# A hybrid encoder layer: the last quarter's upper MLP layer by seven products of eight, with w_down's sums made a pass earlier on GpSimd

## The chip, the cores and the metric

The kernel runs on one core of one Trainium2 chip. The metric is the device time of one execution in microseconds (us), lower is better. The engines are named as in the profile: PE (TensorE matmul), PEld (its weight load), DVE (VectorE), ACT (ScalarE), POOL (GpSimd) and SP (SyncE, which here only issues DMAs).

## The reference, cut to what matters

One encoder layer on x of 2048 tokens by 1024 features, float32: an attention and a convolution side by side, a cross-attention to 256 memory rows, an MLP, a last norm.

```python
h = x + concat([dilated_attention(q, k, v), conformer_conv(a, g)]) @ w_out   # q,k,v,a,g = rmsnorm(x) @ w_in
h = h + cross_attention(rmsnorm(h), rmsnorm(mem)) @ w_xo
u = rmsnorm(h) @ w_up                  # 1024 -> 4096
h = h + square(relu(u)) @ w_down       # 4096 -> 1024
return rmsnorm(h)
```

## The kernel before

All large products run in float16 with each operand split into a high and a low part, so that one product is three matmuls (`mm3`, which is why three neighbouring lines, L374 to L376, hold nearly all of PE's time).

The tokens are cut into four quarters of 512 columns. `post(p)` is the work on quarter p: the output projection, the cross-attention, the MLP and the output; this text calls it a pass, first (p = 0) to last (p = 3). Beside passes 0 to 2, `weave` puts in the attention (`att`) and the convolution (`conv`, DVE's long chain of L391) of the next quarter. The passes are generators; a scheduler then sets the order in which each engine's instructions stand, and every engine takes its queue strictly in that order.

The MLP goes over eight groups (`fg`) of 512 hidden features. The upper layer (w_up) has two forms:
- plain: for each 128 features, 8 x 3 matmuls of 512 columns, 96 in a group (`hidden` in the last pass);
- `quad`: the group as a two by two block product by seven products instead of eight, 7 x 2 x 4 x 3 = 168 matmuls of 256 columns. It needs sums of blocks of w_up and of the activations. The activations' sums are made by `put_columns` when the cross-attention ends. Those of w_up are made once by `prep`, split in float16 and kept in DRAM (`ust`).

Before, groups 5 to 7 of the second pass and all groups of the third use `quad`; the last pass uses the plain form. `prep` runs as a side of the second and third pass (tables `preps`): for each group and each half j it loads two raw pieces of w_up (`pw`, 512 KB each) into buffers that the attention's result has left, makes four sums of 128x512 on DVE, splits everything (`hi` on ACT, `lo` on DVE) and writes the parts (`pt`) to DRAM. It is advanced by one step for each step of the main generator (rate 1.0).

The lower layer (w_down) of the last pass also goes by seven products (`seven`) for groups 0 to 6, with the hidden features' sums made by `parts` and w_down's sums (`sums`, on DVE, 128x1024) and splits (`piece`, ACT and DVE) made anew inside the last pass. In the other passes it is plain, with split weights that the first pass kept in DRAM (`wst`).

POOL does small jobs: the power function in each norm (`nr`, L347), the joining of the three attention patterns, and some DMA issues.

Of the kernel before, what the change touches and what calls it, by code (L numbers as in the profile page):

```python
# [21 lines left out]
P = 128  # L22
# [19 lines left out]
GV = {"mix": 0, "x": 8, "mlp": 16, "final": 24, "conv_b": 32, "ln_g": 36, "ln_b": 40}  # L42

# [5 lines left out]
def hybrid_layer(ctx, tc, A, out):  # L49
# [70 lines left out]
    ust = [[dr.tile([P, 2 * 1024], F16, name=f"ust{fg}_{i}") for i in range(7)] for fg in range(8)]  # L120
    vscr = dr.tile([P, 2, 8, 256], F16, name="vscr")
# [1392 lines left out]
    def prep(fgs):  # L1514
# [11 lines left out]
        def hi(o, i):  # L1526
            ACT.activation(o, i, AF.Copy, scale=S_UP)

        def lo(o, i, h):
            DVE.scalar_tensor_tensor(o, i, S_UP, h, op0=ALU.mult, op1=ALU.subtract)  # L1530

        for fg in fgs:
            for j in range(2):
# [3 lines left out]
                for i in range(2):  # L1537
                    dma(raw[i], wcols(w_up, (4 * fg + 2 * i + j) * P))
                a11, a12, a21, a22 = (r[:, 4 * i:4 * i + 4] for r in raw for i in range(2))
                yield  # L1540
# [4 lines left out]
                DVE.tensor_tensor(s1, a21, a22, op=ALU.add)  # L1545
                DVE.tensor_tensor(a21, a11, a21, op=ALU.subtract)
# [4 lines left out]
                DVE.tensor_tensor(a11, s1, a11, op=ALU.subtract)  # L1551
# [4 lines left out]
                DVE.tensor_tensor(a12, a12, a11, op=ALU.subtract)  # L1556
# [22 lines left out]
    preps = {1: (5, 6, 7, 3), 2: (4, 0, 1, 2)}  # L1579
# [46 lines left out]
    def quad(p, fg, src, hh, rsb):  # L1626
# [21 lines left out]
        def done(e, pt, i, z):  # L1648
# [5 lines left out]
            a, b = (t[:, 2 * i:2 * i + 2, 256 * z:256 * z + 256] for t in hh)  # L1654
            ACT.copy(a, e3)
            DVE.tensor_tensor(b, e3, a, op=ALU.subtract)  # L1656

        X, Y, Z = (ps(f"u{x}", "up") for x in "xyz")
# [16 lines left out]
        Y = ps("uy", "up")  # L1675
# [8 lines left out]
    def post(p):  # L1684
# [70 lines left out]
        if p in preps:  # L1755
            one, two_, src = columns(p)
            put = put_columns(one, two_, hs)
            y = None
        else:
            y = ytiles("m")  # L1760
# [15 lines left out]
        if p == 2:  # L1776
            opened = hidden_tiles(0, order[0])
            opened = (opened, quad(p, order[0], src, opened, rsb))
            next(opened[1])
        r = rstd_from(ssum)  # L1780
# [6 lines left out]
        if p == NG - 1:  # L1787
            last_mlp(hs, y, rsb)
            return
        for g in range(FG // 2):  # L1790
# [3 lines left out]
            for i, fg in enumerate(fgs):  # L1794
# [6 lines left out]
                if src and (p == 2 or fg > 4):  # L1801
                    while fg not in ready:
                        next(prepping[p])
                    yield from main_quad or quad(p, fg, src, ht, rsb)
# [59 lines left out]
    def last_mlp(hs, y, rsb):  # L1864
# [3 lines left out]
        banks.update(up=(4, 5, 6, 7), ux=(0, 1), uy=(2, 3), tr=(0, 1, 2, 3))  # L1868
# [225 lines left out]
```

## Time and profile before

| what | us |
|---|---|
| median of 3 runs | 2685.7 (2682.28 to 2688.09) |
| the profiled execution, whole | 2687.11 |
| its span, first to last instruction | 2685.3 |
| PE busy in the span | 2613.5 |
| DVE busy | 1982.5 |
| ACT busy | 1245.2 |
| POOL busy | 226.2 |

A row of a group of instructions reads: line, engine, operation, out<-in by the program's names, shapes, count, then busy time, mean ns of one, and the idle time before them. A row of a window reads: from and to, its length, and for each engine busy time and count, then granted clock, share of DMA engines in use and GB/s.

### The profile page before, as it was taken

To read this page: it belongs to the slowest core of one execution; us is meant where nothing else is said; L and a number is where in the kernel's file an instruction comes from. 1 tells how busy PE (TensorE), PEld (TensorE's weight loads), DVE (VectorE), ACT (ScalarE), POOL (GpSimd) and SP (SyncE) were. 2 spreads that over 40 slices of the span, in tenths; PEclk is the share of its full clock that TensorE was granted. 3 is DMA by queue.
4 is the path that set the end of the run, shared out by engine and by line. 5 is a ranking of instruction groups with operands and counts; after the bars stand their busy time and mean duration, and the time that the engine had idled before them with its cause. 6 is when DMAs were issued, how large, how long until landed. Compare 5 with 4: busy or idle time off the path is not lost.

```text
span 2685.3 us, 43789 instructions
## 1 busy us (share of the span) xinstructions
PE 2613.5 (97%) x16786; PEld 1561.7 (58%) x16786; DVE 1982.5 (74%) x3816; ACT 1245.2 (46%) x2189; POOL 226.2 (8%) x285
## 2 busy tenths in 40 slices
PE   8999999999899999999999999999999999999998
PEld 7844448766454555445576676555776565444443
DVE  5886656567679996556799985468999755677976
ACT  5637544476454345334552343256443343443433
POOL 1234002132001011100000000000000000000000
PEclk9999999999999999999999999999999999999999
DMA  9977978665526777855357777454787765323331
GB/s 270 296 259 215 286 227 268 176 194 169 164 85 180 231 218 217 267 183 166 118 161 227 216 233 235 126 159 124 234 272 255 232 227 157 102 71 102 114 114 63
DMA packets 445634, 510.97 MB, mean 190 GB/s; under 512 B 89613, under 2 KB 341441, under 8 KB 444656
## 3 DMA queue, kind: packets, MB, share of 16 engines
q1 hardware_dynamic: 438016, 493.15, 60.1%
q10 hardware_dynamic: 5184, 9.01, 0.9%
q0 software_dynamic: 2224, 6.01, 0.6%
q8 instruction: 132, 2.16, 0.3%
q14 instruction: 78, 0.64, 0.1%
HBM read 376.59 MB, written 131.48 MB: 189 GB/s over the span
## 4 chain that ended last, share of the span: by engine, by line
PE 75%; DVE 12%; DMA 6%; issue 3%; ACT 3%; SPq 1%; POOL 1%; DVEq 0%; POOLq 0%; ACTq 0%
PE dn L376 7%; PE dn L375 7%; PE dn L374 7%; PE up L374 6%; PE up L376 6%; PE up L375 6%; PE lin L376 3%; PE lin L374 3%; PE lin L375 3%; DVE cacc L391 3%; PE xs L375 2%; PE xs L376 2%; PE xs L374 2%; PE pt L1030 2%; PE x L375 2%
## 5 line engine op out<-in xcount | busy, mean ns | idle before, releaser
L391 DVE SCALAR_TENSOR_TENSOR cacc<-cu,cw,cacc 128x512 f32<-128x512 f32 x480 | 365.8, 768 | 5.0
L375 PE MATMUL dn<-hhl,ws_d 128*128 128x512 f16 x768 | 291.6, 380 | 1.4 <-DVE hhl L1656 1.1
L376 PE MATMUL dn<-hhh,ws_d 128*128 128x512 f16 x768 | 291.6, 380 | 0.0
L374 PE MATMUL dn<-hhh,ws_d 128*128 128x512 f16 x768 | 288.9, 380 | 1.0 <-ACT hhh L1821 0.4
L374 PE MATMUL up<-mh,ws_u 128*128 128x512 f16 x512 | 194.1, 380 | 0.9 <-ACT mh L1509 0.9
L375 PE MATMUL up<-ml,ws_u 128*128 128x512 f16 x512 | 194.5, 380 | 0.0
L376 PE MATMUL up<-mh,ws_u 128*128 128x512 f16 x512 | 194.4, 380 | 0.0
L1024 ACT ACTIVATE sm<-sm,o 128x256 f32<-128x256 f32 (+1 forms) x288 | 119.4, 455 | 130.7 <-DVE o L1023 130.2
L1023 DVE CUSTOM_DVE_ANT_0 sm<-s,mask,qks 128x256 f32<-128x256 f32 (+1 forms) x384 | 151.9, 436 | 34.4 <-PE s L1064 33.7
L1034 DVE TENSOR_TENSOR pl<-pt,ph 128x512 f16<-128x512 f32 x160 | 110.1, 688 | 41.2 <-ACT ph L1033 40.5
L1838 DVE SCALAR_TENSOR_TENSOR h<-dn,bd,h 128x512 f32<-128x512 f32 x96 | 71.7, 749 | 78.6 <-PE dn L376 76.9
L376 PEld LDWEIGHTS <-ws_d 128*128 128x128 f16 x768 | 75.3, 98 | 90.9 <-issue 2.1
L1033 ACT CAST ph<-pt 128x512 f16<-128x512 f32 x160 | 91.4, 572 | 77.7 <-PE pt L1030 77.5
L375 PEld LDWEIGHTS <-ws_d 128*128 128x128 f16 x768 | 75.2, 98 | 83.3 <-issue 0.8
L374 PEld LDWEIGHTS <-ws_d 128*128 128x128 f16 x768 | 75.3, 98 | 82.6 <-issue 0.7
L376 PEld LDWEIGHTS <-ws_u 128*128 128x128 f16 x832 | 81.7, 98 | 64.0 <-issue 0.6
L375 PEld LDWEIGHTS <-ws_u 128*128 128x128 f16 x832 | 81.6, 98 | 61.6 <-issue 0.9
L374 PEld LDWEIGHTS <-ws_u 128*128 128x128 f16 x832 | 81.6, 98 | 60.9 <-issue 0.6
L1030 PE MATMUL pt<-ident,sm 128*128 128x128 f32 x640 | 99.4, 277 | 9.0 <-DVE catl L1200 4.2
L376 PE MATMUL o<-cath,ws_o 128*128 128x512 f16 x256 | 97.3, 383 | 4.8 <-DVE ws_o L362 4.8
L1030 PEld LDWEIGHTS pt<-ident,sm 128*128 128x128 f32 x640 | 79.2, 143 | 35.0 <-ACT sm L1024 4.2
L374 PE MATMUL o<-cath,ws_o 128*128 128x512 f16 x256 | 97.3, 382 | 0.8 <-ACT cath L1199 0.7
(556 smaller groups left out, 7296.4 us busy)
## 6 DMA issues: line engine op xcount, KB each, us to landing
ws_t<-ust SPq DMA_DIRECT2D x77, 512.0 KB
ws_d<-wst SPq DMA_DIRECT2D x64, 512.0 KB
ws_u<-wst SPq DMA_DIRECT2D x52, 512.0 KB
ust<-pt SPq DMA_DIRECT2D x48, 512.0 KB
raw_d<-in_w_down_dram SPq DMA_DIRECT2D x36, 512.0 KB
scan<-in_w_up_dram SPq DMA_DIRECT2D x32, 512.0 KB
scan<-in_w_down_dram SPq DMA_DIRECT2D x32, 512.0 KB
raw_o<-in_w_out_dram SPq DMA_DIRECT2D x32, 512.0 KB
```

Of the source, the lines that this page charges most:

```text
L374: PE.matmul(o, lh, rh, start=first, stop=False, skip_group_check=more)
L375: PE.matmul(o, lh, rl, start=False, stop=False, skip_group_check=more)
L376: last["pe"] = PE.matmul(o, ll, rh, start=False, stop=end, skip_group_check=more)
L391: DVE.scalar_tensor_tensor(acc, u[:, t:t + 512], cw[:, c, t:t + 1], acc, op0=ALU.mult, op1=ALU.add)
L1023: last["dve"] = DVE.tensor_tensor_reduce(dst, so, mask[:, 256 * m:256 * m + nk], SCORE, 3e38, ALU.add, ALU.min, mn)
L1024: last["act"] = ACT.activation(dst, dst, AF.Exp, bias=mn, scale=-1.0)
L1030: last["pe"] = PE.transpose(pt[:, j, :], sm[:, j, :], ident)
L1033: ACT.copy(ph, pt)
L1034: DVE.tensor_tensor(pl, pt, ph, op=ALU.subtract)
L1838: last["dve"] = DVE.scalar_tensor_tensor(hs[m], pt, K_DN, hs[m], op0=ALU.mult, op1=ALU.add)
```

## The change

- The last pass's upper layer uses `quad` for all eight groups, and so `put_columns` on its activations. What `quad` does with each finished block of hidden features is now a function that it is given (`sink`): `into` writes them as before, and `blocks` in the last pass makes the blocks' sums and splits for `seven` at once.
- In the last pass the first two products of the next group's `quad` are written ahead of `seven`, the other five behind it.
- For groups 0, 2, 4 and 6 (`DOWN`) w_down's sums and their float16 parts are made by `down` as further steps of `prep` in the second and third pass and kept in DRAM (`dst`); `seven` then loads seven ready tiles. For groups 1, 3 and 5 it makes them itself as before.
- `prep`'s loads are issued from POOL's queue instead of SP's, all its sums run on POOL instead of DVE, each half has one more step between load and use, and it advances by 1.5 steps for each main step.

```diff
+DOWN = (0, 2, 4, 6)
...
+    dst = {fg: [dr.tile([P, 2 * 1024], F16, name=f"dst{fg}_{i}") for i in range(7)] for fg in DOWN}
...
+        def both_parts(t, x, i):
+            hi(t[:, 0, x], i, S_DN)
+            lo(t[:, 1, x], i, t[:, 0, x], S_DN)
+        def down(fg, j):
+            nm = f"d{fg}{j}"
+            raw = [ct0.tile([P, 2, 512], F32, tag=f"ch{i}", name=f"pw{i}_{nm}") for i in range(2)]
+            step()
+            for i in range(2):
+                dma(raw[i].rearrange("p h c -> p (h c)"), w_down[(4 * fg + 2 * i + j) * P:(4 * fg + 2 * i + j + 1) * P], POOL)
+            b00, b01, b10, b11 = (r[:, h] for r in raw for h in range(2))
+            def keep(t, *ns):
+                for x, n in enumerate(ns):
+                    give(dst[fg][n].rearrange("p (e j c) -> p e j c", e=2, j=2)[:, :, j], t[:, :, x])
+            yield
+            yield
+            step()
+            s1 = sw.tile([P, 512], F32, tag="s1", name=f"ps1_{nm}")
+            POOL.tensor_tensor(s1, b11, b01, op=ALU.subtract)
+            POOL.tensor_tensor(b01, b01, b00, op=ALU.subtract)
+            t0 = ct0.tile([P, 2, 2, 512], F16, tag="cl0", name=f"pt0_{nm}")
+            both_parts(t0, 0, b00)
+            yield
+            step()
+            both_parts(t0, 1, b01)
+            keep(t0, 0, 3)
+            POOL.tensor_tensor(b00, b11, b01, op=ALU.subtract)
+            yield
+            step()
+            t1 = ct0.tile([P, 2, 2, 512], F16, tag="cl1", name=f"pt1_{nm}")
+            hi(t1[:, 0], raw[1], S_DN)
+            lo(t1[:, 1], raw[1], t1[:, 0], S_DN)
+            keep(t1, 1, 5)
+            POOL.tensor_tensor(b10, b10, b00, op=ALU.subtract)
+            yield
+            step()
+            t3 = sw.tile([P, 2, 1, 512], F16, tag="s4", name=f"pt3_{nm}")
+            both_parts(t3, 0, s1)
+            keep(t3, 4)
+            yield
+            step()
+            t2 = ct0.tile([P, 2, 2, 512], F16, tag="cl0", name=f"pt2_{nm}")
+            both_parts(t2, 0, b00)
+            both_parts(t2, 1, b10)
+            keep(t2, 2, 6)
...
+            if type(fg) is tuple:
+                for j in range(2):
+                    yield from down(fg[0], j)
+                step()
+                continue
...
-                    dma(raw[i], wcols(w_up, (4 * fg + 2 * i + j) * P))
+                    dma(raw[i], wcols(w_up, (4 * fg + 2 * i + j) * P), POOL)
...
+                yield
...
-                DVE.tensor_tensor(s1, a21, a22, op=ALU.add)
-                DVE.tensor_tensor(a21, a11, a21, op=ALU.subtract)
+                POOL.tensor_tensor(s1, a21, a22, op=ALU.add)
+                POOL.tensor_tensor(a21, a11, a21, op=ALU.subtract)
...
-                DVE.tensor_tensor(a11, s1, a11, op=ALU.subtract)
+                POOL.tensor_tensor(a11, s1, a11, op=ALU.subtract)
...
-                DVE.tensor_tensor(a12, a12, a11, op=ALU.subtract)
+                POOL.tensor_tensor(a12, a12, a11, op=ALU.subtract)
...
-    preps = {1: (5, 6, 7, 3), 2: (4, 0, 1, 2)}
+    preps = {1: (5, 6, 7, 3, (DOWN[0],), (DOWN[1],)), 2: (4, 0, 1, 2, (DOWN[2],), (DOWN[3],))}
...
+    def into(hh):
+        def sink(e, i, z):
+            a, b = (t[:, 2 * i:2 * i + 2, 256 * z:256 * z + 256] for t in hh)
+            ACT.copy(a, halved(e))
+            DVE.tensor_tensor(b, halved(e), a, op=ALU.subtract)
+        return sink
...
-    def quad(p, fg, src, hh, rsb):
+    def quad(p, fg, src, sink, rsb):
...
+            sink(e, i, z)
+        X, Y, Z = (ps(f"{'q' if p == NG - 1 else 'u'}{x}", "up") for x in "xyz")
...
-        if p in preps:
+        if p:
...
+        elif p == NG - 1:
+            mlp = last_mlp(hs, src, rsb)
+            next(mlp)
...
-            last_mlp(hs, y, rsb)
+            yield from mlp
...
-        banks.update(up=(4, 5, 6, 7), ux=(0, 1), uy=(2, 3), tr=(0, 1, 2, 3))
+        banks.update(qx=(4,), qy=(7, 5), qz=(6,), ux=(0, 1), uy=(2, 3), tr=(0, 1, 2, 3))
...
+        def blocks(fg):
+            q = {}
+            def sink(e, i, z):
+                q[i, z] = e
+                if z == i or i:
+                    split({(0, 0): A1, (1, 1): A22, (1, 0): A12}[i, z], halves(e))
+                    return
+                DVE.tensor_tensor(q[0, 0], q[0, 0], e, op=ALU.subtract)
+                DVE.tensor_tensor(e, e, q[1, 1], op=ALU.add)
+                DVE.tensor_tensor(q[1, 1], q[1, 1], q[0, 0], op=ALU.subtract)
+                split(S2, halves(q[1, 1]))
+                split(S1, halves(e))
+                DVE.tensor_tensor(q[1, 0], q[1, 0], q[1, 1], op=ALU.subtract)
+                split(S3, halves(q[0, 0]))
+                split(S4, halves(q[1, 0]))
+            return quad(p, fg, src, sink, rsb)
...
-        def piece(w, name):
-            return two(split_to(wtile(name, 4, (P, 2, 512)), w, S_DN))
+        def piece(w, n, name):
+            t = ct0.tile([P, 2, 2, 512], F16, tag=("ch0", "ch1", "cl0", "cl1")[n % 4], name=f"ws_{name}")
+            return two(split_to(t, w, S_DN))
...
+                if b:
+                    wh, wl = piece(b[w], n, f"d{p}{fg}_{n}") if n else first
+                    if n == 1:
+                        DVE.tensor_tensor(b[1, 0], b[1, 0], b[4], op=ALU.subtract)
+                else:
+                    t_ = wtile(f"d{p}{fg}_{n}", 7, (P, 2, 512))
+                    dma(flat(t_), dst[fg][n])
+                    wh, wl = two(t_)
...
+        gen = blocks(0)
+        next(gen)
+        yield
+        for n in range(8):
+            to_rows(n)
+            if n % 2 and n < 7:
+                next(gen)
+        nb = nfirst = None
         for fg in range(FG - 1):
+            b, first = nb, nfirst
+            nb, nfirst, todo = None, None, []
+            if fg < FG - 2 and fg + 1 not in DOWN:
+                nb = {4: room(4, "b")}
+                for z in range(2):
+                    for h in range(2):
+                        nb[z, h] = quarter(fg + 1, z, h)
+                todo = [lambda w=nb[0, 0], n=fg + 1: piece(w, 0, f"d{p}{n}_0")] + sums(nb)
+            if fg == FG - 2:
+                hh = [xquad(q, 1, f"hh{q}") for q in "hl"]
+                gen = quad(p, fg + 1, src, into(hh), rsb)
+            else:
+                gen = blocks(fg + 1)
+            next(gen)
+            nfirst = seven(fg, b, first, todo)
+            for _ in range(3):
+                next(gen)
         fg = FG - 1
...
-                sides.append((prepping[p], 1.0))
+                sides.append((prepping[p], 1.5))
```

What this does to the queues, in three places. First POOL at the start of the second pass's MLP; `nr` is the power function of a norm, `pw0_51` and `pw1_51` are the raw pieces of group 5, half 1, `ps1` a sum. Before:

```order
L347 TENSOR_TENSOR nr_13911<-st_v_13912,mhalf_250 128x4
L1273 COPY o1_20_13788<-low1_20_13789 128x8
L347 TENSOR_TENSOR nr_14995<-st_v_14996,mhalf_250 128x4
L1273 COPY o1_21_14726<-low1_21_14727 128x8
L1273 COPY o1_22_15973<-low1_22_15974 128x8
```

and in the changed kernel:

```order
L351 TENSOR_TENSOR nr_15023<-st_v_15024,mhalf_278 128x4
L1611 TENSOR_TENSOR pw0_50_15096<-ps1_50_15171,pw0_50_15096 128x512
L1616 TENSOR_TENSOR pw0_50_15096<-pw0_50_15096 128x512
L61 DMA pw1_51_15514<-in_w_up_dram 128x8x128
L1605 TENSOR_TENSOR ps1_51_15599<-pw1_51_15514 128x512
L61 DMA pw0_51_15513<-in_w_up_dram 128x8x128
L1606 TENSOR_TENSOR pw1_51_15514<-pw0_51_15513,pw1_51_15514 128x512
L1277 COPY o1_21_14754<-low1_21_14755 128x8
L1611 TENSOR_TENSOR pw0_51_15513<-ps1_51_15599,pw0_51_15513 128x512
L1616 TENSOR_TENSOR pw0_51_15513<-pw0_51_15513 128x512
```

Where POOL had single short jobs, each half now puts two loads and four sums in its queue; the second load stands behind a sum that waits for the first.

Next ACT at the end of the third pass, where the last group's `quad` ends (`e122` to `e422` are its four kept blocks, `hhh2_2` the hidden features that the lower layer reads). Before:

```order
L1653 ACTIVATE e422_24140<-e422_24140 128x512
L1655 CAST hhh2_2_24018<-e422_24140 128x2x256
L1653 ACTIVATE e322_24181<-e322_24181 128x512
L1655 CAST hhh2_2_24018<-e322_24181 128x2x256
L1653 ACTIVATE e222_24114<-e222_24114 128x512
L1655 CAST hhh2_2_24018<-e222_24114 128x2x256
```

and in the changed kernel (`pt0_d61` to `pt3_d61` are parts of w_down's group 6, half 1):

```order
L1722 ACTIVATE e422_24396<-e422_24396 128x512
L1531 ACTIVATE pt0_d61_24472<-pw0_d61_24331,bd_291 128x512
L1690 CAST hhh2_2_24262<-e422_24396 128x2x256
L1722 ACTIVATE e322_24437<-e322_24437 128x512
L1531 ACTIVATE pt1_d61_24516<-pw1_d61_24332,bd_291 128x1024
L1690 CAST hhh2_2_24262<-e322_24437 128x2x256
L1531 ACTIVATE pt3_d61_24522<-ps1_d61_24469,bd_291 128x512
L1722 ACTIVATE e222_24370<-e222_24370 128x512
L1531 ACTIVATE pt0_d61_24472<-pw0_d61_24331,bd_291 128x512
L1690 CAST hhh2_2_24262<-e222_24370 128x2x256
```

Four splits of `down` now stand between the casts that the lower layer waits for; the one of `pt3_d61` reads a sum from POOL.

Last DVE in the last pass, from the end of group 1's `quad` to the start of its `seven` (`e131` to `e431` are the kept blocks, `hql` and `hz` the low parts that `seven` reads, `e132` is the next group's). Before, the same place of group 4 read:

```order
L1888 TENSOR_TENSOR hql_25660<-rl_26999,hqh_25659 128x512
L1888 TENSOR_TENSOR hz10_25664<-rl_26759,hz00_25661 128x512
L1925 TENSOR_TENSOR rl_26956<-rl_26956,rl_26759 128x256
L1888 TENSOR_TENSOR hz11_25665<-rl_26917,hz01_25662 128x512
L1899 SCALAR_TENSOR_TENSOR rl_27044<-up_27019,ssumx3_25326 128x512
L1925 TENSOR_TENSOR rl_26999<-rl_26999,rl_26917 128x256
L1974 SCALAR_TENSOR_TENSOR rowsh_25653<-dn_27047,bd_263,rowsh_25653 128x512
```

and in the changed kernel:

```order
L1718 TENSOR_TENSOR e231_26499<-e231_26499,up_26287 128x512
L1958 TENSOR_TENSOR hql_25979<-e331_26555,hqh_25978 128x2x256
L1720 SCALAR_TENSOR_TENSOR e231_26499<-e231_26499,ssumx3_25608 128x512
L1979 TENSOR_TENSOR e131_26316<-e131_26316,e231_26499 128x512
L1980 TENSOR_TENSOR e231_26499<-e231_26499,e431_26525 128x512
L1958 TENSOR_TENSOR hql_25979<-e131_26316,hqh_25978 128x512
L1981 TENSOR_TENSOR e431_26525<-e431_26525,e131_26316 128x512
L1958 TENSOR_TENSOR hz11_25984<-e231_26499,hz01_25981 128x512
L1718 TENSOR_TENSOR e132_26664<-e132_26664,up_26634 128x512
L1984 TENSOR_TENSOR e331_26555<-e331_26555,e431_26525 128x512
L1958 TENSOR_TENSOR hz10_25983<-e431_26525,hz00_25980 128x512
L2041 SCALAR_TENSOR_TENSOR rowsh_25972<-dn_26690,bd_291,rowsh_25972 128x512
```

The hidden features' sums, which stood between four plain pieces, now form one run behind the last block of `quad`.

93 lines of the change are left out of this document (23 added, 70 removed).

## The prediction

> **What bounds the kernel now.** I read the page first, then the busy times of the stretches that the change touches, then who PE waits for there.
>
> ```profile
> PE 2613.5 (97%) x16786; PEld 1561.7 (58%) x16786; DVE 1982.5 (74%) x3816; ACT 1245.2 (46%) x2189; POOL 226.2 (8%) x285
> PE 75%; DVE 12%; DMA 6%; issue 3%; ACT 3%; SPq 1%; POOL 1%; DVEq 0%; POOLq 0%; ACTq 0%
> ```
>
> PE is the bound, with 97% of the span and 75% of the chain that ended last. So time is won by fewer matmul columns, and lost wherever another engine makes PE wait. By stretches (the MLP of the second, of the third and of the last pass, and the tail):
>
> ```profile
> core 0: us, PE busy (x) PEld busy (x) DVE busy (x) ACT busy (x) POOL busy (x), PEclk, DMA share, GB/s
> 1340.00:1640.00 300.00, 297.91 (x2299) 208.13 (x2298) 261.21 (x490) 115.59 (x199) 3.88 (x5) 0.99 0.68 207
> 1840.00:2160.00 320.00, 314.65 (x2399) 217.19 (x2397) 289.34 (x547) 143.22 (x250) 3.77 (x5) 1.00 0.75 241
> 2380.00:2640.00 260.00, 258.99 (x1198) 116.84 (x1197) 219.54 (x319) 100.67 (x143) 0.00 (x0) 1.00 0.33 104
> ```
>
> In the last pass PE is idle for 1.0 us of 260: matmuls taken out there come off the end, as long as the new order keeps PE fed. In the second and third pass, where `prep` grows, PE is idle for 2.1 of 300 and 5.3 of 320 us, but DVE has only 38.8 and 30.7 us left and POOL is empty. PE's largest wait from the second pass's MLP to the third's (us in all, number, the largest):
>
> ```profile
> PE up L374 <- ACT e L1645: 6.5, 2, 5.7
> ```
>
> **The last pass's matmuls.** A row is start, duration, engine, line. The first two are the ends of 24 neighbouring matmuls of 256 columns in the third pass's `quad`, the last two the ends of 52 neighbouring plain ones of 512 columns in the last pass.
>
> ```profile
> 1905.97 0.27 PE L374 MATMUL up<-T4h,ws_t 128*128 128x256 f16 x1
> ...
> 1908.48 0.27 PE L376 MATMUL up<-T4h,ws_t 128*128 128x256 f16 x1
> ...
> 2414.01 0.38 PE L375 MATMUL up<-ml,ws_u 128*128 128x512 f16 x1
> ...
> 2425.01 0.38 PE L375 MATMUL up<-ml,ws_u 128*128 128x512 f16 x1
> ```
>
> Start to start, (1908.48 - 1905.97) / 23 = 0.1091 us against (2425.01 - 2414.01) / 51 = 0.2157 us: half the columns cost a little over half. A group falls from 96 x 0.2157 = 20.71 to 168 x 0.1091 = 18.33 us, so 2.38 us less, and eight groups give **-19.0 us**. `seven` keeps its 84 matmuls of 512 columns.
>
> **Does the last pass stay fed?** DVE loses work there:
>
> ```profile
> L362 DVE SCALAR_TENSOR_TENSOR ws_d<-b,bd,ws_d 128x1024 f16<-128x1024 f32 x40 | 51.3, 1284 | 7.9 <-ACT ws_d L361 7.9
> L1952 DVE TENSOR_TENSOR b<-b,b 128x1024 f32<-128x1024 f32 x12 | 14.7, 1222 | 0.0
> L1649 DVE TENSOR_TENSOR e<-e,up 128x512 f32<-128x512 f32 x26 | 17.7, 685 | 0.5 <-ACT e L1645 0.5
> ```
>
> Each of the groups 0, 2, 4 and 6 drops 7 splits of 1.28 and 4 sums of 1.22 us, 13.8 us; four groups, 55 us. Against it each group gets four additions of a kept block (0.685, the third row) and its sums become 11 operations of 512 elements where they were smaller: I make it 13.1 us a group against 11.4, so 8 x 1.7 = 14 us more. DVE falls by some 41 us in a pass that shortens by 19: from 84% to about 74%. The tight place is the run behind the last block (the last of the rows on the order): eight DVE operations of 0.69 us and ACT's square, some 6 us, until `hz10` is there, which `seven` reads in its third product. Ahead of that PE has two products of the next `quad` (48 x 0.1091 = 5.2) and `seven`'s first two (24 x 0.2157 = 5.2): 10.4 us of cover, so I take nothing from it, but 1 us for the first group, where no `seven` stands between. If DVE lags by over 4 us at the seam, the excess is paid seven times. Loads grow from 104 GB/s by 28 + 14 - 16 - 8 = 18 MB in 240 us to about 180 GB/s, below the 241 of the third pass: hidden.
>
> **What `prep` costs DVE in the second and third pass.** The prices of one operation (by form, second pass), and of ACT's half:
>
> ```profile
> L1530 DVE SCALAR_TENSOR_TENSOR pt<-pw,bd,pt 128x1024 f16<-128x1024 f32 x16 | 20.5, 1281 | 0.0
> L1530 DVE SCALAR_TENSOR_TENSOR pt<-pw,bd,pt 128x512 f16<-128x512 f32 x16 | 12.0, 750 | 0.0
> L1545 DVE TENSOR_TENSOR ps<-pw 128x512 f32<-128x512 f32 x8 | 5.5, 687 | 0.0
> L1527 ACT ACTIVATE pt<-pw,bd x32: 705/928/1152, 1363.5 to 1627.5; 128x1024 f16<-128x1024 f32 x16, 128x512 f16<-128x512 f32 x16
> ```
>
> Per pass DVE gives away 8 halves x 4 sums x 0.69 = 22 us. It gets 4 halves of w_down x (5 x 0.75 + 1.28) = 20 us of splits; ACT gets 4 x (5 x 0.71 + 1.15) = 19 us on an engine that is busy 39 to 45%. So the count alone is even. But the sums do not vanish: 32 + 16 = 48 of them now run on POOL beside DVE. What that does shows where the first pass joins attention patterns on POOL:
>
> ```profile
> 956.53 0.69 DVE L1822 TENSOR_TENSOR hhl<-rl,hhh 128x512 f16<-128x512 f32 x1
> 957.13 1.54 DVE L391 SCALAR_TENSOR_TENSOR cacc<-cu,cw,cacc 128x512 f32<-128x512 f32 x2
> ...
> 960.17 1.04 POOL L1186 TENSOR_TENSOR ld<-ld,ce 128x512 f32<-128x512 f32 x1
> 960.25 2.04 DVE L362 SCALAR_TENSOR_TENSOR ws_u<-raw_u,bd,ws_u 128x1024 f16<-128x1024 f32 x1
> 961.17 2.02 POOL L1186 TENSOR_TENSOR cat<-o,ce 128x512 f32<-128x512 f32 x1
> 962.82 0.92 DVE L391 SCALAR_TENSOR_TENSOR cacc<-cu,cw,cacc 128x512 f32<-128x512 f32 x1
> 963.16 1.49 POOL L1186 TENSOR_TENSOR ld<-ld,ce 128x512 f32<-128x512 f32 x1
> 963.66 1.53 DVE L1822 TENSOR_TENSOR hhl<-rl,hhh 128x512 f16<-128x512 f32 x1
> 964.72 3.10 POOL L1189 TENSOR_TENSOR cat<-cat,ld 128x512 f32<-128x512 f32 x2
> 965.12 3.25 DVE L391 SCALAR_TENSOR_TENSOR cacc<-cu,cw,cacc 128x512 f32<-128x512 f32 x2
> ...
> 1064.75 2.47 POOL L1189 TENSOR_TENSOR cat<-cat,ld 128x512 f32<-128x512 f32 x2
> 1066.39 2.47 DVE L439 TENSOR_TENSOR lc<-lc,lrc 128x512 f32<-128x512 f32 x4
> ```
>
> Beside POOL the split of 1024 takes 2.04 instead of 1.28, `hhl` 1.53 instead of 0.69, two `cacc` 3.25 instead of 1.54, one 0.92 instead of 0.77: 3.5 us lost over five POOL sums, **0.70 us each**. The four `lc` (one operand in PSUM) lose nothing. So a sum on POOL costs DVE between 0 and 0.70 us; most of DVE's time in these passes is two-operand work like `cacc` and the splits, but not all, so I take 0.5: 48 x 0.5 = 24 us per pass (0 to 34). [...]
>
> Net, DVE gets 20 - 22 + 24 = +22 us per pass (-2 to +32), into 38.8 us of slack in the second pass and 30.7 in the third. That fits on average, but DVE ends at 94 and 97%. What PE loses when DVE is that full:
>
> ```profile
> 1900.00:2000.00 100.00, 99.01 (x796) 71.18 (x795) 98.22 (x183) 41.57 (x74) 0.44 (x1) 1.00 0.82 265
> 2000.00:2100.00 100.00, 97.54 (x753) 66.98 (x751) 94.65 (x177) 40.16 (x71) 0.44 (x1) 1.00 0.75 243
> ```
>
> 1.0 and 2.5 us in 100. At 2 in 100 over 620 us PE would be idle for about 12 us where it is now idle for 7.4: +5. To it I add +2 for the end of the third pass, where four splits now stand on ACT between the casts that the lower layer waits for, and +1 for POOL's queue, where the loads now wait in front of `nr`: **+8 us** in all, from -5 (the 5.7 us wait above goes) to +25.
>
> **POOL's queue.** A load from POOL lands, by its DMA issues (median, in us):
>
> ```profile
> oscr<-o POOLq DMA_DIRECT2D x19, 264.0 KB, 4.4
> v<-vtok POOLq DMA_DIRECT2D x2, 260.0 KB, 7.8
> ```
>
> Twice these bytes: I estimate 6 to 10 us. A half's chain is then the second load 8, four sums at 1.3 of which three follow each other 4, and two rounds of splits on ACT and DVE 7: 19 us, where the pass offers 300 / 12 = 25. It holds, with little to spare. SP's queue loses the loads' waits and gets `dst`'s writes (7 MB per pass, as `late` one step after they are made): at 207 and 241 GB/s with a share of 0.68 and 0.75, 11 MB more is about 0.1 of share; hidden.
>
> **The sum.** -19.0 + 1 + 8 = -10.0 us. The profiled execution took 2687.1 us, 1.4 above the median, inside the runs' spread of 5.8. From the median of 2685.7 the forecast is **2676 us**. About 0.2% (5 us) is what a measurement here can tell from no change.
>
> **The rivals.**
> - *POOL's sums fill DVE* (slower). In the third pass 30.7 us of slack and 2 us of even count give 32.7 / 48 = 0.68 us per sum as the point where DVE is full; the measured 0.70 in the thick batch lies just at it. At 1.04 us (the sum's whole time) DVE gets 48 us per pass: 9 over in the second, 17 over in the third, all of it PE's. With the 8 and the 1 from above that is -19 + 35 = +16: 2702 us; a sum at 0.85 gives about 2692. For it: DVE stands at 98% in 1900 to 2000 already. Against: a good part of DVE's operands lie in PSUM. [...] Chance 0.27.
> - *POOL's loads pace `prep`*: at 10 us a load and with both loads in turn a half takes over 25 us, ACT and DVE stand in their queues before splits whose data is late, and PE with them; 2 us on each of 16 late halves is +32 - 19 = 2699. The trace has ACT waiting for such a load before, though from SP. Chance 0.07.
> - *The last pass stalls at each seam*: 2 us on seven groups, and the 8 us: 2690. Against it are DVE's 26% idle. Chance 0.06.
> - *All is covered*: -19 and up to 5 of the wait at the end of the second pass: 2662 to 2667. Chance 0.15.
> - The forecast: 0.45, with 2668 to 2684 as its own range.
>
> **Numbers.** The range of 2663 to 2702 leaves out the best of the fully covered case and the worst of the two POOL cases. Faster than 0.2%: 0.15 + 0.39 of the forecast's 0.45 + 0.03 = 0.57. Slower: 0.25 + 0.04 = 0.29. Within: 0.14.
>
> **What would show it.** The last pass: `up` rows of 256 columns at 0.109 us start to start, PE idle below 4 us from the cross-attention's end to the last output, DVE near 74%. Passes two and three: `cacc` and `pt` rows stretched beside POOL sums, 0.5 us lost per sum, PE idle for about 15 us. I am wrong if PE is idle for over 30 us in passes two and three, if POOL's loads need over 10 us, or if PE waits for `hz` in the last pass.

## The result, and the profile after

The changed kernel takes **2707.2 us** (median of 4 runs, 2701.4 to 2708.5) against 2684.7 us before: ratio 1.0079, 95% interval 1.006 to 1.0097. It is slower by 0.8%; the forecast was 2676. The profiled execution took 2708.0 us with a span of 2706.2. Its page (span, busy time of each engine):

```profile
span 2706.2 us, 45365 instructions
PE 2607.6 (96%) x17362; PEld 1623.7 (60%) x17362; DVE 2009.8 (74%) x3767; ACT 1268.6 (47%) x2236; POOL 412.1 (15%) x429
```

PE is still the bound, but its busy time fell by 5.9 us only, where the forecast for the shorter matmuls was 19. Where the time lies is read from the length of each MLP, from the last residual row of cross-attention to the last row that adds a `dn` product (in the last pass, to PE's last row). The kernels on which the cause rests are in the table.

| kernel | median us | ratio to before | second MLP | third MLP | last MLP |
|---|---|---|---|---|---|
| before | 2684.7 | | 369.3 | 351.8 | 319.2 |
| after | 2707.2 | 1.0079 | 373.3 | 384.8 | 302.3 |
| e1 sums on VectorE | 2688.5 | 1.0011 | 364.3 | 369.4 | 301.2 |
| e2 loads on SyncE's queue | 2698.5 | 1.0053 | 370.8 | 378.8 | 302.6 |
| e3 no w_down parts in third pass | 2705.0 | 1.0074 | 371.9 | 381.8 | 302.5 |
| e4 the same, pace 1.0 | 2697.6 | 1.0043 | 373.8 | 372.6 | 302.7 |
| f1 the same, pace 1.2 | 2688.0 | 1.0015 | 371.9 | 365.3 | 300.2 |
| f2 before, sums on GpSimd | 2694.9 | 1.0037 | 365.7 | 359.2 | 319.2 |
| g2 no sums | 2670.4 | 0.9954 | 362.1 | 360.1 | 300.4 |
| g3 sums unused | 2703.9 | 1.0077 | 372.6 | 380.2 | 300.4 |
| g4 sums of 16 columns | 2673.5 | 0.9962 | 363.1 | 356.9 | 302.7 |
| g5 sums unused, loads on SyncE | 2695.6 | 1.0039 | 373.9 | 375.1 | 302.2 |
| c5 parts in the first pass's tail and the second | 2667.8 | 0.9943 | 367.3 | 350.1 | 301.0 |

So the last MLP did what it should (16.9 us shorter), the second lost 4.0 us, and the third lost **33.0 us**. The stretches of after that answer to those of before:

```profile
1340.00:1640.00 300.00, 294.77 (x2271) 205.82 (x2270) 270.78 (x470) 121.75 (x211) 77.90 (x63) 0.99 0.72 224
1840.00:2160.00 320.00, 294.31 (x2166) 198.92 (x2165) 289.50 (x496) 135.71 (x237) 74.50 (x56) 0.96 0.72 227
2420.00:2660.00 240.00, 240.00 (x1632) 159.47 (x1631) 174.22 (x244) 76.36 (x113) 0.00 (x0) 1.00 0.55 169
```

In the last MLP PE is never idle in 240 us and DVE is 73% busy. In the third pass PE is idle for 25.7 of 320 us, its granted clock is 0.96 there, and DVE is busy for 289.5 us, just as before. From the second pass's MLP to the third's, PE waits mostly for ACT's copy out of the `up` bank and for DVE rows of `quad` (us in all, number, longest):

```profile
PE up L378 <- ACT e L1714: 18.4, 6, 5.5
PE dn L378 <- DVE e L1718: 4.4, 4, 2.3
PE up L378 <- DVE e L1718: 3.9, 2, 3.1
PE up L378 <- DVE h L1908: 3.1, 2, 2.6
```

Cut at the MLP's own seams (its first three quarters, then the last), before reads:

```profile
1871.00:2143.40 272.40, 267.05 (x2062) 186.27 (x2061) 250.07 (x469) 112.28 (x196) 3.77 (x5) 1.00 0.76 242
2143.40:2222.80 79.40, 79.40 (x540) 52.82 (x538) 44.84 (x79) 31.05 (x48) 0.00 (x0) 1.00 0.63 215
```

and after:

```profile
1875.10:2177.80 302.70, 277.01 (x2062) 190.00 (x2061) 268.06 (x453) 120.13 (x208) 81.32 (x61) 0.96 0.74 236
2177.80:2259.90 82.10, 80.12 (x540) 52.77 (x538) 56.88 (x87) 38.71 (x60) 14.11 (x12) 1.00 0.84 282
```

The same 2062 matmuls take 302.7 instead of 272.4 us in the first three quarters. Of the third MLP's 33 us, idle time of PE is 22.3 (27.7 against 5.4) and longer busy time of PE is 10.7 (357.1 against 346.5 for the same matmuls). The second part is mostly the clock: for 18.0 us of PE's busy time in the third MLP the granted clock was 0.50 (before: for none) and matmuls of 256 columns came 0.213 instead of 0.109 us apart, so 9 us of the 10.7. Four windows of 4 us around the end (at 1989.1 us) of a wait of 5.55 us:

```profile
1984.00:1988.00 4.00, 0.00 (x0) 0.00 (x0) 1.99 (x5) 1.53 (x4) 1.02 (x1) 0.70 0.82 182
1988.00:1992.00 4.00, 2.90 (x14) 2.08 (x14) 3.91 (x6) 3.57 (x7) 2.64 (x3) 0.50 0.76 173
1992.00:1996.00 4.00, 4.00 (x37) 3.47 (x35) 3.96 (x6) 0.59 (x1) 1.02 (x1) 0.94 0.75 282
1996.00:2000.00 4.00, 4.00 (x48) 3.66 (x46) 4.00 (x10) 1.46 (x3) 0.00 (x0) 1.00 0.77 250
```

PE does nothing, comes back at a granted clock of 0.50 with 14 matmuls in 2.9 us, and is at full pace only 3.4 us after its return (its matmuls come 0.213 us apart from 1989.1 to 1992.5 us, then 0.109). In the first window, while PE stands, DVE and ACT are busy for half of the time or less.

The second pass has the same number of sums and loses much less. Its groups 0 to 4 use the plain form, its groups 5 to 7 `quad`; the changed kernel, cut just before `quad` begins:

```profile
1356.00:1560.00 204.00, 203.23 (x1624) 147.29 (x1623) 192.88 (x329) 76.32 (x133) 56.44 (x44) 1.00 0.70 215
1560.00:1729.30 169.30, 158.78 (x1088) 103.93 (x1086) 118.98 (x206) 75.00 (x121) 33.36 (x31) 0.98 0.78 250
```

In the plain part DVE is 95% busy beside 27 of the sums, and PE is idle for 0.8 us of 204. In the `quad` part DVE is 70% busy, and PE is idle for 10.5 us of 169 (before: 7.6 of 166). So a full DVE alone did not hold up PE; the waits stand where `quad` runs, and in the third pass all groups use it.

What the sums on GpSimd do to DVE stands in the groups. After, over those first three quarters:

```profile
L395 DVE SCALAR_TENSOR_TENSOR cacc<-cu,cw,cacc 128x512 f32<-128x512 f32 x120 | 101.0, 849 | 0.9
...
L1534 DVE SCALAR_TENSOR_TENSOR pt<-pw,bd,pt 128x1024 f16<-128x1024 f32 x16 | 24.7, 1551 | 4.7 <-ACT pt L1531 4.7
...
L1616 POOL TENSOR_TENSOR pw<-pw 128x512 f32<-128x512 f32 x8 | 14.8, 1846 | 0.6
```

and before:

```profile
L391 DVE SCALAR_TENSOR_TENSOR cacc<-cu,cw,cacc 128x512 f32<-128x512 f32 x120 | 88.2, 750 | 0.4
L1530 DVE SCALAR_TENSOR_TENSOR pt<-pw,bd,pt 128x1024 f16<-128x1024 f32 x16 | 20.5, 1282 | 0.2 <-ACT pt L1527 0.2
```

The same 120 `cacc` take 849 instead of 750 ns, a split of 1024 takes 1551 instead of 1282, and the slowest group of GpSimd sums takes 1.85 us in the mean, where the prediction's first POOL row has 1.04. Over all forms of DVE instructions, the time above each form's undisturbed duration (its tenth percentile) is 25.5 us in the second and 32.4 us in the third MLP, against 2.6 and 3.0 before: the difference is 0.48 and 0.61 us for each of 48 sums.

### The profile page after: what moved, and what is told of

Read it like the earlier page. It is cut to its first block, busy times and chain, and to the rows that moved or that the text cites. A ratio compares the mean times of both kernels' runs of the same rounds, so it can differ in the third digit from the quotient of the medians.

```text
span 2706.2 us, 45365 instructions
## 1 busy us (share of the span) xinstructions
PE 2607.6 (96%) x17362; PEld 1623.7 (60%) x17362; DVE 2009.8 (74%) x3767; ACT 1268.6 (47%) x2236; POOL 412.1 (15%) x429
## 5 line engine op out<-in xcount | busy, mean ns | idle before, releaser
L395 DVE SCALAR_TENSOR_TENSOR cacc<-cu,cw,cacc 128x512 f32<-128x512 f32 x480 | 389.8, 815 | 5.8
L379 PEld LDWEIGHTS <-ws_t 128*128 128x128 f16 x1064 | 105.8, 99 | 44.7 <-issue 28.7
L351 POOL TENSOR_TENSOR nr<-st_v,mhalf 128x4 f32<-128x4 f32 (+1 forms) x15 | 14.2, 947 | 765.5 <-DVE st_v L347 415.1
L378 PEld LDWEIGHTS <-ws_t 128*128 128x128 f16 x1064 | 105.8, 99 | 16.3
L380 PEld LDWEIGHTS <-ws_t 128*128 128x128 f16 x1064 | 105.9, 100 | 15.6
L378 PE MATMUL up<-T32h,ws_t 128*128 128x256 f16 x304 | 86.0, 283 | 18.5 <-ACT e L1714 18.4
L380 PE MATMUL o<-cath,ws_o 128*128 128x512 f16 x256 | 97.2, 382 | 4.8 <-DVE ws_o L366 4.8
L1714 ACT COPY e<-up 128x512 f32<-128x512 f32 x76 | 43.7, 579 | 120.3 <-PE up L380 119.9
L378 PE MATMUL up<-mh,ws_u 128*128 128x512 f16 x256 | 97.7, 382 | 0.4 <-ACT mh L1513 0.4
```

Of the source, the lines that this page charges most:

```text
L351: POOL.tensor_tensor(dst, v, mhalf.to_broadcast([P, v.shape[1]]), op=ALU.pow)
L378: PE.matmul(o, lh, rh, start=first, stop=False, skip_group_check=more)
L379: PE.matmul(o, lh, rl, start=False, stop=False, skip_group_check=more)
L380: last["pe"] = PE.matmul(o, ll, rh, start=False, stop=end, skip_group_check=more)
L395: DVE.scalar_tensor_tensor(acc, u[:, t:t + 512], cw[:, c, t:t + 1], acc, op0=ALU.mult, op1=ALU.add)
L1714: last["act"] = ACT.copy(e, pt)
```

## The experiments

**Two theories at first.** A: VectorE is full in the third MLP. B: ScalarE stands in its queue before preparation splits whose data is late, and PE behind its copies. Four kernels, each one edit away from the changed one.

e1 and e2 put one kind of work back:

```diff
-                POOL.tensor_tensor(s1, a21, a22, op=ALU.add)      # e1: all eight sums of prep
+                DVE.tensor_tensor(s1, a21, a22, op=ALU.add)
-                    dma(raw[i], wcols(w_up, (4 * fg + 2 * i + j) * P), POOL)   # e2: all loads of prep
+                    dma(raw[i], wcols(w_up, (4 * fg + 2 * i + j) * P))
```

> The 96 sums of the preparation go back from GpSimd to VectorE; its loads stay on GpSimd's queue. The changed kernel took 2707 us; its third pass's MLP alone lost 33 us. Theory A (VectorE is full there): per pass VectorE gets 48 x 0.69 = 33 us of sums and is rid of the 23 and 29 us that GpSimd's sums cost it, so 4 to 10 us more per pass: 2708 to 2720. Theory B (ScalarE stands in its queue before preparation splits whose data is late, and TensorE waits for its copies): a sum takes 0.69 instead of 1.5 us and stands in no second queue, so the third MLP gets back 10 us or more: 2690 to 2698.

> The 48 loads of 512 KB of the preparation go back from GpSimd's to SyncE's queue; the sums stay on GpSimd. Theory A (VectorE is full): VectorE's work is the same, 2703 to 2711. Theory B (late data in ScalarE's queue): loads no longer wait behind GpSimd's sums, the stalls in the third MLP fall by a third or more: 2690 to 2698; if it is rather SyncE's queue that is late, 2707 or more.

e1 took 2688.5 us (ratio 1.0011, 1.0 to 1.0021): the sums' place is worth 19 us, just below B's range and far from A's 2708 to 2720. e2 took 2698.5 us: GpSimd's queue for the loads is worth 9 us, at the upper edge of B's range.

e3 and e4 take the third pass's w_down parts out, e4 also its denser pace:

```diff
-    preps = {1: (..., (DOWN[0],), (DOWN[1],)), 2: (4, 0, 1, 2, (DOWN[2],), (DOWN[3],))}
+    preps = {1: (..., (DOWN[0],), (DOWN[1],)), 2: (4, 0, 1, 2)}
-                    dma(flat(t_), dst[fg][n])
+                    dma(flat(t_), dst[fg % 4][n])
-                sides.append((prepping[p], 1.5))                       # e4 only
+                sides.append((prepping[p], 1.5 if p == 1 else 1.0))
```

> The third pass prepares no parts of w_down for groups 4 and 6 (the last pass reads those of groups 0 and 2 in their place); the up-parts keep their pace of 1.5 steps. Theory A (VectorE has too little room over the third MLP): 4 halves x 5 us of splits and 16 sums x 0.6 = 30 us of VectorE time go, more than the 25 that were added: the third MLP falls back from 385 to about 355 us, 2677 to 2682. Theory B (late data at this pace): the stalls lie in the first two thirds of the third MLP, where the up-parts are made at the same pace as before this edit, so they stay: 2695 to 2705.

> As e3 (no parts of groups 4 and 6 made in the third pass, those of 0 and 2 read instead), with the third pass's preparation at 1.0 step instead of 1.5, as in the kernel before. Theory A (room on VectorE over the whole MLP): the same as e3. Theory B (late data at the denser pace): the stalls go only here: 2675 to 2682, 15 us or more below e3.

e3 took 2705.0 us: without the new parts nearly nothing comes back, so they are not what the third MLP pays for. e4 took 2697.6, 7 us less, not the 15 that B asked for. The first three quarters of the third MLP, e1, e3 and e4 in turn:

```profile
1867.30:2147.20 279.90, 268.39 (x2046) 184.97 (x2045) 258.98 (x481) 117.06 (x200) 18.23 (x22) 0.99 0.79 253
```

```profile
1873.50:2176.00 302.50, 278.01 (x2062) 190.29 (x2061) 259.28 (x442) 111.74 (x196) 66.62 (x49) 0.96 0.70 224
```

```profile
1876.10:2149.30 273.20, 267.28 (x2064) 186.14 (x2061) 247.64 (x435) 106.70 (x188) 55.47 (x43) 1.00 0.72 230
2149.30:2248.70 99.40, 83.97 (x539) 54.49 (x538) 54.08 (x82) 37.01 (x55) 8.57 (x6) 0.91 0.62 204
```

e1 and e3 have the same DVE time, 259.0 and 259.3 us, but e1 loses 7.5 us against before's 272.4 (its window ends 16 matmuls early, which is 3.5 us at most) and e3 loses 30.1: the total of DVE's work does not decide, GpSimd's sums at this pace do. The rest of e1's 17.6 us lies in its last quarter, where the w_down parts are made. At pace 1.0 (e4) the first three quarters lose 0.8 us; there the last quarter pays 20 us instead. PE waits 14.8 us in it for `ws_t`, loaded from the copies in `ust`; presumably the slower pace stores these too late. f1 goes between:

```diff
+                sides.append((prepping[p], 1.5 if p == 1 else 1.2))    # on e3
```

> As e3 and e4 (third pass makes no parts of groups 4 and 6, those of 0 and 2 are read instead), with the third pass's preparation at 1.2 steps. Each up-half has 6 steps instead of the 5 of before, so 1.2 gives it the time that it had before. In e4 (1.0) the first three quarters of the third MLP were as fast as before and the last lost 20 us waiting for copies of the last group that were made too late; in e3 (1.5) the first three quarters lost 30. Theory B (the stalls come from the denser pace, with GpSimd's sums in the chain): both go, third MLP 350 to 360 us, 2676 to 2684. Rival C (the chain with GpSimd is too slow for any pace that meets the deadlines): 2693 or more.

f1 took 2688.0 us, 4 above B's range; third MLP 365.3: the last quarter is as before (79.4 us), the first three lose 13.5. So the loss of the first three quarters grows with the pace: 0.8, 13.5 and 30 us at 1.0, 1.2 and 1.5. f2 is the kernel before with the GpSimd sums alone (`DVE.tensor_tensor` becomes `POOL.tensor_tensor` in `prep`):

> The kernel before with one part of the change alone: its 64 up-sums on GpSimd, pace, loads and the rest as before. VectorE is rid of 32 x 0.69 = 22 us per pass and loses 32 x 0.5 to 0.6 = 16 to 19 us to GpSimd's reads. Theory B (only the denser pace made the chain late): 2682 to 2690. Rival C (sums on GpSimd make the splits late at any pace): 2695 to 2705.

f2 took 2694.9 us (1.0037, 1.0024 to 1.005), slower than B allowed, at the low edge of C: the third MLP lost 7.4 us although DVE gave 22 us of sums away. So GpSimd's sums cost time at the pace of before too.

**By which way?** Either GpSimd's sums lengthen the DVE instructions beside them, or the sums are late for those who wait. g1 and g2 take the sums out of the chain; g1 keeps them on GpSimd, adding constants into a scratch tile:

```diff
-                POOL.tensor_tensor(a21, a11, a21, op=ALU.subtract)     # each sum; the splits take the raw blocks
+                POOL.tensor_tensor(s1, mask[:, 0:512], mask[:, 512:1024], op=ALU.add)   # g1; no line in g2
```

> The changed kernel with its 96 sums taken out of the preparation's chain: GpSimd adds two constant tiles into a scratch tile instead, as often and of the same size, and the splits take the raw blocks (so the prepared weights are other numbers). Nobody waits for a sum any more, but GpSimd reads SBUF beside VectorE as before. Theory B1 (the sums' place in the chain makes the splits late): the stalls go, 2676 to 2686, within 5 us of g2. Theory A1 (GpSimd's reads slow VectorE by 0.5 to 0.6 us per sum, and that makes TensorE wait): 2698 to 2707.

> As g1, without any sum: the splits take the raw blocks, GpSimd only starts the loads. Both theories: the stalls of the third MLP go but for what loads and stores cost at this pace; third MLP 355 to 365 us, 2674 to 2684. What g1 loses against it is the price of GpSimd's reads, what the changed kernel loses against g1 is the price of waiting for sums.

g2 took 2670.4 us, 37 below the changed kernel. g1 took 2710.9, but does not answer the question: its sums waited for nothing and ran in the first pass (81 GpSimd additions between 740 and 976 us, where before has 26), and there the time was lost: the first MLP ended 37 us later, the third took 358.2 us. It shows something else, in a chain of short DVE instructions that ran beside these additions. The last scaling of the softmax, in g1:

```profile
L1787 DVE TENSOR_SCALAR xp<-xp,xdn 128x256 f32<-128x256 f32 x16 | 16.2, 1060 | 0.1
```

and before:

```profile
L1720 DVE TENSOR_SCALAR xp<-xp,xdn 128x256 f32<-128x256 f32 x16 | 4.8, 349 | 0.1
```

Three times as long, for an operation with a single tile as input. A single pair, in the changed kernel: a GpSimd sum ran from 1975.96 to 1977.65 us, and the `cacc` that started beside it at 1976.45 took 1.75 us; the `cacc` of 1974.46, with no sum beside it, took 0.75. g3 and g4 repeat the test in place: in g3 each sum reads the loaded blocks but writes a scratch tile that nobody reads, in g4 each sum is waited for but adds 16 columns.

```diff
-                POOL.tensor_tensor(a21, a11, a21, op=ALU.subtract)
+                POOL.tensor_tensor(s1, a11, a21, op=ALU.subtract)                                         # g3
+                POOL.tensor_tensor(a22[:, 0, 0:16], a11[:, 0, 0:16], a21[:, 0, 0:16], op=ALU.subtract)     # g4
```

> The changed kernel; its 96 sums run on GpSimd at their places and read the loaded blocks, but write a scratch tile that nobody reads, and the splits take the raw blocks (the prepared weights are other numbers). Without any sum (g2) it was 2670 us, with all 2707. Theory (1), GpSimd's reads lengthen VectorE's instructions (0.5 to 0.6 us a sum) and TensorE waits for those: 2698 to 2707. Theory (2), splits wait for late sums: 2670 to 2680. Both by half: about 2688.

> The changed kernel; its 96 sums stay on GpSimd, at their places and waited for as before, but add 16 of 512 columns (the prepared weights are other numbers). Theory (1): the reads are short, so nearly all of the 37 us goes: 2670 to 2678. Theory (2): the hop through GpSimd's queue stays, but not the sum's own 1.5 us: 2685 to 2700.

2703.9 against 2673.5 us. Nobody waits for g3's sums, and it is as slow as the changed kernel, within 3 us; g4's are waited for as in the change, and it is 3 us from the kernel without sums. `cacc` from 1880 to 2180 us, in g3:

```profile
L395 DVE SCALAR_TENSOR_TENSOR cacc<-cu,cw,cacc 128x512 f32<-128x512 f32 x119 | 99.9, 848 | 1.0
```

and g4:

```profile
L395 DVE SCALAR_TENSOR_TENSOR cacc<-cu,cw,cacc 128x512 f32<-128x512 f32 x112 | 82.7, 748 | 1.0
```

In g3 the loads still stood behind the sums in GpSimd's queue. g5 is g3 with the loads on SyncE's queue, as in e2:

> As g3 (full sums on GpSimd at their places, their results unused, splits of the raw blocks), with the preparation's loads on SyncE's queue: neither a split nor a load waits for a sum any more, only the reads stay. Theory (1), the reads alone make TensorE wait: 2692 to 2704, at most the 9 us below g3 that e2 was below the changed kernel. Theory (2b), loads are late behind the sums: 2670 to 2682.

2695.6 us. So of the 37 us between the changed kernel and g2, some 3 are waiting for the sums' results (2707.2 to 2703.9, within the spread), 8 are the loads in GpSimd's queue (to 2695.6; e2 had 9), and **25 are the sums' running beside VectorE alone** (to 2670.4). g2's loads still start on GpSimd, g5's on SyncE; c7 below shows that this choice is worth nothing without sums (2669.6 against c5's 2667.8 us). The third MLP of g5 and then of g2:

```profile
1872.60:2247.70 375.10, 351.55 (x2600) 240.34 (x2598) 324.51 (x538) 158.17 (x267) 73.63 (x49) 0.99 0.78 252
1864.20:2224.30 360.10, 348.61 (x2601) 239.80 (x2598) 295.73 (x540) 158.17 (x267) 20.47 (x27) 1.00 0.81 263
```

DVE has nearly the same number of instructions in both and is busy for 29 us more in g5, and PE is idle for 12 us more. A rival would be that GpSimd's small jobs come late behind the sums in its queue. In g5 DVE waits for one of them once in the second and once in the third MLP (`lcol`, 1.1 and 2.8 us), and in the 20 us behind either PE has no wait over 0.3 us; the stretch between the two MLPs, with the norms, is 145.4 us long, as before. So this is not it. What is left is theory A's agent, GpSimd beside VectorE, without A's condition that VectorE be full. Whether it is the sums' reads of SBUF, as the expectations have it, or their writes was not separated.

Without any sum (g2) the second MLP is 7 us shorter than before and the third still 8 longer. So of the third MLP's 33 us, 25 are the sums, with all that hangs on them, and 8 are the pace and the new splits, loads and stores.

**A version that keeps the gain.** c1 and c2 make all w_down parts in the first pass's MLP and the up-parts as before (c2 with GpSimd's sums and loads for the w_down parts):

```diff
+    preps = {0: ((0,), (2,), (4,), (6,)), 1: (5, 6, 7, 3), 2: (4, 0, 1, 2)}
+            sides.append((prepping[p], (1.0, 1.0, 1.0)[p]))
```

> All parts of w_down for the four groups are made in the first pass's MLP (VectorE 60% busy there from 1000 to 1270 us), with sums on VectorE and loads on SyncE's queue; the up-parts of the second and third pass are made as in the kernel before (5 steps, sums on VectorE, loads on SyncE's queue, 1.0 step). Theory: the last pass keeps the 17 to 18 us that it gained, passes two and three are as before, and the first pass has room for 8 x 7.8 = 62 us of VectorE's and 40 of ScalarE's work: 2665 to 2673. Rival: the first pass's queues stall behind it (its DMA engines are 69% busy): 2680 or more.

> As c1, with the sums for w_down on GpSimd and their loads on GpSimd's queue, as in the change. Theory: VectorE has room in the first pass either way, so the same as c1 within 4 us: 2665 to 2675. Rival C (GpSimd's sums make the chain late wherever they stand): 10 us or more above c1.

2706.3 and 2709.3 us, far above both ranges; c2 is 3 us above c1, as its theory had it, so GpSimd's sums are not what this costs. The second, third and last MLP are as hoped (365.3, 352.0 and 299.8 in c1), but the first pass's MLP, with the residual of its cross-attention, lost 36 us. The parts began with it, where DVE had little room before:

```profile
840.00:940.00 100.00, 95.91 (x539) 49.16 (x538) 95.63 (x153) 39.76 (x60) 11.83 (x14) 0.97 0.71 209
940.00:1040.00 100.00, 100.00 (x587) 51.76 (x586) 86.20 (x139) 43.94 (x67) 12.11 (x13) 1.00 0.77 225
```

c3 and c4 use other places:

```diff
+    preps = {0: ((0,), (2,)), 1: (5, 6, 7, 3), 2: (4, 0, 1, 2), 3: ((4,), (6,))}   # c3; in c4 (0,), (2,) stand in 1
+                weave(islice(main, 45), *sides)                      # first pass: parts from step 45 on
+                sides.append((prepping[p], 0.8))
```

> The parts of w_down are made where VectorE is at 55 to 60%: those of groups 0 and 2 in the last third of the first pass's MLP, those of groups 4 and 6 in the last pass ahead of its MLP; sums on VectorE, loads on SyncE's queue. The up-parts of passes two and three are made as in the kernel before. Theory: passes two and three as in c1 (4 us faster than before, no loss), the last MLP 18 us shorter, 2 to 6 us lost where the parts are made: 2664 to 2674. Rival: these stages are latency-bound chains (statistics, softmax) and stall as the first pass did in c1: 2680 to 2695.

> As e1 (sums on VectorE, loads on GpSimd's queue), with the third pass's parts of w_down moved to the last pass ahead of its MLP and the third pass's pace at 1.2. e1 lost 8 us in the first and 10 in the last quarter of its third MLP against before. Theory: the last quarter's loss goes with the parts, the first quarter's mostly with the pace; the stage where they are made loses 1 to 3: 2668 to 2678. Rival as for c3: 2682 or more.

2689.5 and 2687.0 us: the rival. In c3 the last third of the first MLP took the two groups for nothing, but in both kernels the last pass ahead of its MLP lost 20 and 23 us (from the last `o` residual to the last cross-attention residual 109.5 and 112.4 us, before 89.7). In c3 ACT stands there for 19.4 us in front of splits whose buffer is still being stored to `dst`, and PE waits for the softmax, which stands in ACT's queue with them:

```profile
PE x L378 <- ACT xp L1782: 4.5, 1, 4.5
PE ptx L1793 <- DVE ptl L1796: 3.3, 2, 3.0
PE xs L378 <- ACT xp L1782: 2.8, 1, 2.8
```

c5 and c6 leave that place out:

```diff
+    preps = {0: ((0,), (2,)), 1: (5, 6, 7, 3, (4,), (6,)), 2: (4, 0, 1, 2)}        # c5, pace 0.8 / 1.5 / 1.2, sums on DVE
+    preps = {0: ((0,), (2,), (4,), (6,)), 1: (5, 6, 7, 3), 2: (4, 0, 1, 2)}        # c6, from step 45, pace 1.4
```

> Parts of w_down for groups 0 and 2 in the last third of the first pass's MLP (in c3 that cost nothing: 366.6 us for that MLP against 368.4), those for groups 4 and 6 in the second pass as in e1 (its MLP took 364 against 369 us), none in the third; all sums on VectorE, loads on GpSimd's queue, pace 1.2 in the third pass (353 us in c4 against 352). Theory (VectorE's room decides): 2685 - 18 (last MLP) - 5 + 1 = 2663, 2660 to 2668. Rival: a stage pays for it that showed no loss alone: 2675 or more.

> All parts of w_down in the last third of the first pass's MLP (62 us of VectorE's time where about 73 are free between 1040 and 1210 us), up-parts made as in the kernel before. Theory: it just fits, 2662 to 2672. Rival: VectorE is full there, and the head of the second pass, a chain, is late: 2678 or more.

**c5 took 2667.8 us**, ratio 0.9943 (0.9931 to 0.9956): faster than both kernels and at the upper edge of its range (the second MLP gave 2 us, not 5). c6 took 2715.7, the rival's side: four groups in that third are too many. The first MLP took 382.8 us instead of 368.4, and the parts were not done when it ended at 1223 us: the last split starts on ACT at 1243.5 us, in c5 at 1191.6. From the end of that MLP to the last `o` residual c6 took 86 us instead of 54. VectorE, which the rival had full in that third, was busy for 75% (1040 to 1130 us) and 78% (1130 to 1223 us) of it. The stage from the end of the MLP in c6, at a granted clock of 0.82:

```profile
1223.00:1309.00 86.00, 70.38 (x337) 36.74 (x337) 43.13 (x79) 31.66 (x50) 1.01 (x1) 0.82 0.56 174
```

c5's busy times in the first pass's tail, and the first three quarters of its third MLP:

```profile
1040.00:1125.00 85.00, 85.00 (x495) 43.34 (x494) 61.64 (x96) 46.82 (x68) 12.03 (x16) 1.00 0.84 264
1125.00:1208.00 83.00, 83.00 (x390) 38.19 (x389) 62.19 (x80) 42.03 (x56) 13.40 (x16) 1.00 0.95 303
...
1870.70:2140.40 269.70, 266.20 (x2055) 185.46 (x2053) 249.96 (x469) 111.48 (x196) 15.62 (x18) 1.00 0.76 244
```

PE has no idle time in the tail with DVE at 73 to 75% and the DMA engines at 0.84 and 0.95. c7 is c5 with the loads on SyncE's queue:

> c5 (2668 us) with the preparation's loads on SyncE's queue. If GpSimd's queue and its own work on each load (0.9 us) cost something also without sums: 2660 to 2665; if SyncE's queue is the tighter one: 2670 or more; else 2666 to 2670.

2669.6 us, the same as c5 within the spread: without full-length sums on GpSimd, its queue is no worse for these loads than SyncE's.

## Why the prediction was wrong

- **The last pass: right.** -19.0 + 1 was forecast; its MLP took 302.3 instead of 319.2 us, -16.9. The pitch is as forecast, two rows 23 matmuls apart (start, duration):

```profile
2420.04 0.27 PE L378 MATMUL up<-B2h,ws_t 128*128 128x256 f16 x1
...
2422.55 0.27 PE L380 MATMUL up<-B2h,ws_t 128*128 128x256 f16 x1
```

(2422.55 - 2420.04) / 23 = 0.109 us. PE waits once in that MLP (2.0 us for `ws_d`), never for `hz`; the seams stalled nowhere.

- **The price of a GpSimd sum for DVE: right.** 0.5 us was taken, 0.48 and 0.61 were measured. Both sides grow: `cacc` takes 849 instead of 750 ns, and the slowest group of GpSimd sums 1.85 us in the mean, where the five sums between 1340 and 2260 us with no DVE instruction beside them took 1.25 to 1.27. No run shows sums that cost DVE 1.04 us each, the term of rival 1; 0.48 and 0.61 us in the mean stand in its place.
- **"That fits on average", and the +8 us for PE that was built on it: the step that failed.** The prediction set +22 us per pass against 30.7 us of slack in the third pass and charged PE 2 in 100. First, the slack was read from the wrong stretch: 1840 to 2160 holds 31 us ahead of the MLP, while in the three quarters in which the up-parts are made 22.3 us were free (272.4 - 250.1), and pace 1.5 with 6 steps a half crowds them there by a quarter. Second, slack was the wrong measure: e3 lost 30 us with DVE at 86%, e1 lost 7.5 at 93%, and the plain groups of the second MLP lost less than 1 us at 95%. PE lost where `quad` runs and GpSimd's sums stand beside DVE: +8 was forecast for both passes, +4.0 and +33.0 were measured. That the lengthened DVE instructions come late, in order, for the banks and stores that ACT and PE wait for, is the reading that fits; no run follows one such delay from end to end.
- **A term was missing: the clock.** 10.7 of the third MLP's 33 us are longer busy time of PE, 9 of them from half pace (a granted clock of 0.50) behind its five waits of 2.3 to 5.6 us; the sum charged a wait its own length only.
- **Rival 1, "POOL's sums fill DVE" (0.27): its agent was right, its condition not.** Its worst case, 2702, came nearest to the result, but by luck: it was to decide at 0.68 us a sum and put the worst at 1.04, with DVE overfull. The sums cost 0.61, DVE was not full, and the time was lost all the same. This rival did not count the clock either; the result is 5 us above its worst case and out of the range.
- **Rival 2, the loads: small.** They landed in 7.0 and 7.5 us (6 to 10 was estimated), and their queue cost 8 to 9 us, not 32. The w_down parts in the third pass, the largest addition there, cost 2 us (e3).

How exactly a lengthened instruction becomes a wait of PE (through ACT's buffers, SyncE's stores or DVE's own order) differs from wait to wait, and was not separated. Why the `quad` groups wait and the plain ones do not, and what exactly holds up the head of c6's second pass, is open too.

## What to carry to other kernels

Work moved from VectorE to GpSimd was not work removed here: a sum of 0.69 us on VectorE still cost it 0.48 to 0.61 us in the mean from GpSimd. Where TensorE waits closely for VectorE, price each GpSimd instruction by what it does to the instructions beside it, and test it by running it with its result unused. Read slack from the very stretch into which the work goes, and look at how densely it is woven there; but a busy share did not say here whether the waits reach TensorE (30 us lost at 86% in e3, less than 1 us at 95% in the plain groups). Here half of the new work in a stretch with VectorE at 57%, and the other half in the second pass, all on VectorE, kept the last pass's gain (17 of 18 us, c5). All of it in that stretch (c6), or half of it beside a short chain (c3, c4), lost more than it won.

## What the runs showed of the hardware

TensorE fell to half pace behind waits of 2 to 6 us here. In the second and third MLP of the changed kernel, behind each of the seven waits of 2.3 to 5.6 us, the granted clock was 0.50 and matmuls of 256 columns came 0.213 us apart (those of 512 columns 0.43) for 2.8 to 5.1 us, at once or up to 1.3 us later; then they came 0.109 us apart (0.216) again. Behind the five waits of 1.1 to 1.8 us none did. The longest wait alone does not decide: in the same trace two waits of 1.26 and 0.62 us, ending at 629.56 and 630.57 us, were followed by half pace (to 633.95 us), and a single one of 1.83 us, ending at 1660.13, was not.

DVE instructions with one tile as input were longer beside GpSimd's additions as well: 1060 against 349 ns for the `TENSOR_SCALAR` rows of the softmax in g1.
